# Seven-product gates in the convolution branch of a hybrid layer, between two halves of the attention branch's merging

## The chip, the cores and the metric

The kernel runs on one core of a Trainium2 chip. The metric is the device time of one execution in microseconds; the median of three runs before the change is 881.17 us. A core has TensorE (PE, matrix products, with its weight loads as PEld), VectorE (DVE), ScalarE (ACT), GpSimd (POOL), and SyncE (SP), which here only issues transfers.

## The reference

One layer on 512 positions of width 1024 (float32). Four branches read the normed input through one projection, each is gated by a sigmoid of 1024 more columns of that projection, and their sum goes through `w_o`; a gated feed-forward part with 2816 channels follows.

```python
h = rms_norm(x, mix_norm)
sc_b, sc_c, sc_x, pool_in, conf_in, q, k, v, gate_logits = split(h @ w_in)
y_sc = (sc_b * causal_dwconv(sc_c * sc_x, sc_conv)) @ sc_out
y_pool = pool_mixer(pool_in, pool_w, pool_scale)
y_conf = silu(layer_norm(causal_dwconv(a * sigmoid(g), conf_conv) + conf_conv_b, ln_g, ln_b)) @ conf_out   # a, g = split(conf_in)
y_diff = diff_attention(q, k, v, ...) @ diff_out
gates = sigmoid(gate_logits).reshape(b, s, 4, D_MODEL)
x = x + sum_i(gates_i * y_i) @ w_o
x = x + (silu(c_gate) * c_up) @ w_down      # c_gate, c_up = causal_dwconv(rms_norm(x) @ w_up)
```

## The kernel before

Activations lie transposed, 128 channels by 512 positions a tile. Each matrix operand is held as a rounded high part and the rest, and `mm3` (L181) makes one product in three: high by high, high by low (of the activation), low by high (of the weight).

**Weights.** All weights stand in one stream in the order of their use, cut into pieces of 128 x 1024 (eight 128 x 128 blocks). `fetch` (L116) loads a piece with SyncE's queue into a raw buffer, `load_chunk` (L130) splits it: ScalarE casts the high part (L144, `wh`), VectorE subtracts for the low part (L145, `wl`). Raw pieces have two buffers, split ones three, and pieces are split two ahead of use (`AHEAD`). `step` (L158) counts one unit for each block used; `at` and `after` put small work at a unit, and each `step` runs what is due.

**Seven products.** The down projection multiplies pairs of row blocks by pairs of column blocks with seven products in place of eight. The left operands are blocks of the weights (`a12, a11, a22`, from `wa`) and four sums of blocks, which GpSimd's queue adds up in DRAM with accumulating transfers (`make_sums`, L218: per group of four pieces one copy of 1 MB, then additions of 1 MB, 512 KB and 256 KB, each waiting for the one before). Such a piece ("s") has 896 columns and is loaded by two transfers, into tiles `ra` and `rb` of their own. The right operands are halves of 256 positions and combinations of them (`operands`, L707). `seven` (L729) runs the seven products of each pair, and VectorE adds the results (L755 to L758).

**Order.** TensorE's list: branch C's input, q, k, v; then the short convolution's inputs with attention's scores between; the pool inputs (GpSimd adds up windows, L567); then the four branches are merged one after the other. For branch s and d, each of eight output tiles takes `mixed` (12 products from four blocks) and `gate` (24 products of 512 columns); branch p takes 3 and 24. Branch C's 8 gates come before its outputs, 24 products each (L656), kept until its eight `mixed` (L658). Then `w_o`, and twice the feed-forward part: up projections (10, then 12 channel blocks) and the seven-product down projection.

**Between.** Branch C's convolution has 31 taps on four tiles, 124 VectorE operations (`tap`, L384, tile `cacc`) spread by units over TensorE's list. After gate 2 of branch C has begun what is left of them is issued, then `norm_mean` (L630) and, at gate 4, `norm_out` (L641): the mean and variance over channels are column sums that TensorE makes with a tile of ones (`colsum`, L319, two products each). The Tile scheduler sets each engine's list from this program order; GpSimd's is the program's order (`MANUAL`).

Of the kernel before, what the change touches and what calls it, by code (L numbers as in the profile page):

```python
# [15 lines left out]
P = 128  # L16
# [30 lines left out]
SUMU = 30  # L47
DEEP = 2
LOG_EXP = "natural_log_exp_and_others"
# [7 lines left out]
NTMP = 13  # L57
# [21 lines left out]
def hybrid_layer_kernel(ctx: ExitStack, tc: tile.TileContext, xT: bass.AP, w: bass.AP, cols: bass.AP, wa: bass.AP,  # L79
# [36 lines left out]
    def fetch(i, pieces=1):  # L116
        kind, c = plan[i]
        if kind == "s":
            g, o = divmod(c, GRP)
            ra, rb = m2(f"ra{i}", F32), m2(f"rb{i}", F32)  # L120
            nc.sync.dma_start(ra[:, :AW], wa[c])
            nc.sync.dma_start(rb, sums[g][:, o * SW:(o + 1) * SW])
            return ((slice(0, AW), ra[:, :AW]), (slice(AW, AW + SW), rb))
        raw = wp.tile([P, CW], F32, tag="raw", name=f"wr{i}", bufs=2)
        cuts = [slice(i * CW // pieces, (i + 1) * CW // pieces) for i in range(pieces)]
        for s in cuts:
            nc.sync.dma_start(raw[:, s], w[c][:, s])
        return tuple((s, raw[:, s]) for s in cuts)
# [89 lines left out]
    def make_sums():  # L218
# [11 lines left out]
        for g in range(len(sums)):  # L230
# [88 lines left out]
    def colsum(total, name):  # L319
        a = tsplit(total, name)  # L320
# [137 lines left out]
    after(QLAG, lambda: kT.extend(qk_heads("k", krows, col("k_norm"))))  # L458
    vps = time_major("v")
# [77 lines left out]
    def sc_in(j):  # L537
# [6 lines left out]
        u = padded(f"u{j}", 2)  # L544
# [44 lines left out]
    after(SUMU, make_sums)  # L589
# [33 lines left out]
    for m in range(KD):  # L623
        py = mixed(m, "d", ydiff)
        merge(m, py, gate(m, "d"))

# [3 lines left out]
    def norm_mean():  # L630
# [18 lines left out]
    for m in range(KD):  # L649
        if m == 2:  # L650
# [3 lines left out]
        if m == 4:  # L654
            norm_out()
        gates.append(gate(m, "c", True))  # L656
# [33 lines left out]
    H = T // 2  # L690
# [16 lines left out]
    def operands(i, ge, go, homes):  # L707
        def slot(name):
# [9 lines left out]
        nc.vector.scalar_tensor_tensor(  # L718
            out=wt[:, :H], in0=vt[:, :H], scalar=-1.0, in1=b22, op0=ALU.mult, op1=ALU.subtract)
        nc.vector.scalar_tensor_tensor(  # L720
            out=wt[:, H:], in0=wt[:, :H], scalar=-1.0, in1=b21, op0=ALU.mult, op1=ALU.subtract)
        v = split(vt, "", dst=(slot(f"vh{i}"), slot(f"vl{i}")))
        w_ = split(wt, "", dst=(slot(f"wh{i}"), slot(f"wl{i}")))
        left, right = slice(0, H), slice(H, T)
        pick = lambda x, c: (x[0][:, c], x[1][:, c])
        return {"b11": (e[:, left], e[:, right]), "b22": pick(o, left), "b21": pick(o, right), "v1": pick(v, left),
                "t3": pick(v, right), "w2": pick(w_, left), "t4": pick(w_, right)}

    def seven(name, ops):  # L729
        a, b, c, d = (bank(f"{name}{x}") for x in "abcd")  # L730
        r1, r6, r2, r7, r5, r4, r3 = d[:, :H], a[:, :H], a[:, H:], b[:, :H], b[:, H:], c[:, :H], c[:, H:]
        n = len(ops)
        for k, x in enumerate(ops):
            a12, a11, a22, s3_, s1_, s2_, s4_ = blocks7()
            f, l = k == 0, k == n - 1
            mm3(r1, a11, x["b11"], f, l, True)
            mm3(r5, s1_, x["v1"], f, l, True)
            mm3(r6, s2_, x["w2"], f, l, True)
            mm3(r2, a12, x["b21"], False, l, True)
# [154 lines left out]
```

## Time and profile before

| | |
|---|---|
| median of three runs | 881.17 us (880.93 to 881.26) |
| profiled execution | 880.71 us |
| its span | 878.9 us |
| TensorE busy | 871.6 us, 4372 products |
| VectorE busy | 659.3 us |
| ScalarE busy | 404.9 us |
| branch C's gate stretch | 412.35 to 456.88 us |
| first down projection | 631.48 to 681.87 us |

The span is what the profile covers, the rest of the execution lies around it. Busy time counts an instruction from its start to its end; products overlap, so the distance between two starts, and not a product's duration, tells what one costs. A wait is idle time of an engine put down to what ended it. The landing time of a transfer goes from its issue to its arrival.

### The profile page before, as it was taken

The numbers are of one execution on the slowest core, as the hardware profiler recorded it, in microseconds if no ns is written. First come the engines' busy times: TensorE is split into PE (matmuls) and PEld (weight loads), VectorE is DVE, ScalarE is ACT, GpSimd is POOL, SyncE is SP. The second block draws the span as 40 slices with busy tenths as digits, with TensorE's granted clock in tenths as the row PEclk, the third lists the DMA queues.
The fourth block names the chain that finished last, engine by engine and source line by source line (L and its number), as shares of the span: only waits on it lengthen the run. The fifth ranks groups of instructions, "written<-read, shape, count | busy, mean of one in ns | idle before, by whom it ended". The sixth has DMA issues, their size and how long they took to land.

```text
span 878.9 us, 11626 instructions
## 1 busy us (share of the span) xinstructions
PE 871.6 (99%) x4372; PEld 739.0 (84%) x4372; DVE 659.3 (75%) x1091; ACT 404.9 (46%) x636; POOL 71.3 (8%) x101
## 2 busy tenths in 40 slices
PE   9999999999999999999999999999999999999997
PEld 7888888888888888888888888888899888888997
DVE  7399966897957999534468566988886788888865
ACT  7343455464675432222564345444454344444542
POOL 1003300002411101111101100000000000000000
PEclk9999999999999999999999999999999999999999
DMA  6322242222479888888789862323662423334671
GB/s 235 114 96 97 80 123 73 72 97 97 138 200 213 183 215 206 220 216 205 189 208 250 226 157 72 119 97 103 208 178 63 131 98 97 96 106 158 174 210 49
DMA packets 54921, 128.98 MB, mean 147 GB/s; under 512 B 4896, under 2 KB 24352, under 8 KB 54688
## 3 DMA queue, kind: packets, MB, share of 16 engines
q1 hardware_dynamic: 36512, 95.98, 32.9%
q0 software_dynamic: 17776, 31.72, 18.5%
q8 instruction: 34, 0.56, 0.3%
q10 hardware_dynamic: 576, 0.53, 0.2%
q14 instruction: 23, 0.19, 0.1%
HBM read 126.12 MB, written 33.82 MB: 182 GB/s over the span
## 4 chain that ended last, share of the span: by engine, by line
PE 99%; DVE 0%; issue 0%; DVEq 0%
PE fg L182 5%; PE fu L182 5%; PE fg L183 5%; PE fu L183 5%; PE fg L184 5%; PE fu L184 5%; PE gts L182 2%; PE gts L184 2%; PE gts L183 2%; PE gtp L182 2%; PE gtc L182 2%; PE gtp L184 2%; PE gtc L183 2%; PE wo L183 2%; PE wo L182 2%; PE gtd L184 2%
## 5 line engine op out<-in xcount | busy, mean ns | idle before, releaser
L144 ACT CAST wh<-wr 128x1024 fp32r<-128x1024 f32 (+1 forms) x137 | 140.1, 1026 | 199.8 <-PE gtd L183 33.1
L145 DVE TENSOR_TENSOR wl<-wr,wh 128x1024 fp32r<-128x1024 f32 (+1 forms) x137 | 163.4, 1196 | 75.2 <-ACT wh L144 68.6
L391 DVE SCALAR_TENSOR_TENSOR cacc<-glu,colt,cacc 128x512 f32<-128x512 f32 x120 | 89.7, 752 | 1.9
L686 DVE SCALAR_TENSOR_TENSOR fc<-f,colt,fc 128x512 f32<-128x512 f32 x88 | 65.8, 749 | 7.7 <-ACT fc L684 6.4
L182 PE MATMUL fg<-hs,wh 128*128 128x512 f32 x176 | 68.5, 389 | 0.0
L184 PE MATMUL fg<-hs,wl 128*128 128x512 f32 x176 | 68.5, 389 | 0.0
L183 PE MATMUL fg<-hs,wh 128*128 128x512 f32 x176 | 68.5, 389 | 0.0
L182 PE MATMUL fu<-hs,wh 128*128 128x512 f32 x176 | 68.5, 389 | 0.0
L183 PE MATMUL fu<-hs,wh 128*128 128x512 f32 x176 | 68.5, 389 | 0.0
L184 PE MATMUL fu<-hs,wl 128*128 128x512 f32 x176 | 68.5, 389 | 0.0
L144 ACT CAST wh<-ra 128x384 fp32r<-128x384 f32 x44 | 22.6, 513 | 46.8 <-PE dn12c L183 7.6
L684 ACT ACTIVATE fc<-f,colt 128x512 f32<-128x512 f32 x44 | 31.6, 718 | 19.1 <-DVE f L103 16.6
L184 PEld LDWEIGHTS fu<-hs,wl 128*128 128x128 f32 x176 | 33.1, 188 | 6.9
L184 PEld LDWEIGHTS fg<-hs,wl 128*128 128x128 f32 x176 | 33.0, 188 | 6.9
L182 PEld LDWEIGHTS fg<-hs,wh 128*128 128x128 f32 x176 | 33.0, 188 | 6.9
L183 PEld LDWEIGHTS fg<-hs,wh 128*128 128x128 f32 x176 | 33.1, 188 | 6.8
L182 PEld LDWEIGHTS fu<-hs,wh 128*128 128x128 f32 x176 | 33.0, 188 | 6.8
L183 PEld LDWEIGHTS fu<-hs,wh 128*128 128x128 f32 x176 | 33.0, 188 | 6.8
L145 DVE TENSOR_TENSOR wl<-ra,wh 128x384 fp32r<-128x384 f32 x44 | 24.4, 554 | 19.1 <-ACT wh L144 19.0
L681 DVE TENSOR_TENSOR f<-fu,rs 128x512 f32<-128x512 f32 x22 | 15.1, 688 | 20.4 <-PE fu L184 20.4
L145 DVE TENSOR_TENSOR wl<-rb,wh 128x512 fp32r<-128x512 f32 x44 | 30.2, 687 | 0.0
L144 ACT CAST wh<-rb 128x512 fp32r<-128x512 f32 x44 | 27.1, 617 | 0.0
(1673 smaller groups left out, 2375.6 us busy)
## 6 DMA issues: line engine op xcount, KB each, us to landing
wr<-w SPq DMA_DIRECT2D x132, 512.0 KB, 3.3
sums<-s POOLq DMA_DIRECT2D x11, 1024.0 KB, 9.4
rb<-sums SPq DMA_DIRECT2D x44, 256.0 KB, 4.0
ra<-wa SPq DMA_DIRECT2D x44, 192.0 KB, 3.7
sums<-s POOLq DMA_DIRECT2D x11, 512.0 KB, 7.0
sums<-s POOLq DMA_DIRECT2D x11, 256.0 KB, 5.4
x<-xT SPq DMA_DIRECT2D x8, 256.0 KB, 5.6
xin<-xT SPq DMA_DIRECT2D x1, 1024.0 KB, 7.8
```

The source lines that it names most:

```text
L144: nc.scalar.copy(hi[:, s], src)
L145: nc.vector.tensor_tensor(out=lo[:, s], in0=src, in1=hi[:, s].bitcast(F32), op=ALU.subtract)
L182: nc.tensor.matmul(ps, a[0], b[0], start=start, stop=False, skip_group_check=shared)
L183: nc.tensor.matmul(ps, a[0], b[1], start=False, stop=False, skip_group_check=shared)
L184: nc.tensor.matmul(ps, a[1], b[0], start=False, stop=stop, skip_group_check=shared)
L391: nc.vector.scalar_tensor_tensor(out=acc31[j], in0=glus[j][:, i:i + T], scalar=wc, in1=acc31[j], op0=ALU.mult, op1=ALU.add)
L681: nc.vector.tensor_tensor(out=u[:, 2:2 + T], in0=ps, in1=rs, op=ALU.mult)
L684: nc.scalar.activation(c, u[:, 2:2 + T], AF.Copy, scale=col("ffn_conv", o + 2))
L686: nc.vector.scalar_tensor_tensor(out=c, in0=u[:, i:i + T], scalar=col("ffn_conv", o + i), in1=c, op0=ALU.mult, op1=ALU.add)
```

## The change

Branch C's gates are made in pairs by seven products of 256 columns (`gate_pair`), four pairs with four folds each. Their right operands come from the normed input: `fold` adds the high and low parts of two tiles, forms the combinations and splits them; four folds are placed by unit while the pool and attention branches are merged. The weights' sums come from four more groups in DRAM, 15 in place of 11; two of them are issued early, after k's products. All pieces now use the same raw buffers, three in place of two, the folds' sums among them, and one temporary buffer is given up. The edges of the short convolution's tiles are zeroed by VectorE, not GpSimd. In `seven` the first product of the first fold moves to the end of that fold.

The four pairs stand after four of the eight tiles of the attention branch's merging, the other four tiles after them. The mean's sum is issued 22 units after the taps' end, the variance's 14 units after the mean's. The host lays the weights out in this order.

```diff
+EARLY = 2
 DEEP = 2
+STD = 4
+FOLD = 4
+FOLDS = 14
+FOLD0 = -26
+MULAG = 22
+VARLAG = 14
+PLAN = [("n", 57 + 3 * STD // 2)]
+PLAN += [("s", MP * FOLD), ("n", 3 * (KD - STD) // 2 + 4 + 8 + 2 * CUT), ("s", MP * CUT // 2), ("n", 2 * (NP - CUT)), ("s", MP * (NP - CUT) // 2)]
...
-NTMP = 13
+NTMP = 12
...
-    up0 = w.shape[0] - 2 * NP
-    plan = [("n", c) for c in range(up0 + 2 * CUT)]
-    plan += [("s", c) for c in range(MP * CUT // 2)]
-    plan += [("n", c) for c in range(up0 + 2 * CUT, w.shape[0])]
-    plan += [("s", c) for c in range(MP * CUT // 2, MP * NP // 2)]
-    sums = [dram.tile([P, GRP * SW], F32, name=f"sums{g}") for g in range(MP * NP // 2 // GRP)]
+    plan, n_of = [], {"n": 0, "s": 0}
+    for kind, n in PLAN:
+        plan += [(kind, n_of[kind] + i) for i in range(n)]
+        n_of[kind] += n
+    sums = [dram.tile([P, GRP * SW], F32, name=f"sums{g}") for g in range(n_of["s"] // GRP)]
...
         kind, c = plan[i]
+        raw = wp.tile([P, CW], F32, tag="raw", name=f"wr{i}", bufs=3)
         if kind == "s":
             g, o = divmod(c, GRP)
-            ra, rb = m2(f"ra{i}", F32), m2(f"rb{i}", F32)
-            nc.sync.dma_start(ra[:, :AW], wa[c])
-            nc.sync.dma_start(rb, sums[g][:, o * SW:(o + 1) * SW])
-            return ((slice(0, AW), ra[:, :AW]), (slice(AW, AW + SW), rb))
-        raw = wp.tile([P, CW], F32, tag="raw", name=f"wr{i}", bufs=2)
+            n = AW + SW
+            nc.sync.dma_start(raw[:, :AW], wa[c])
+            nc.sync.dma_start(raw[:, AW:n], sums[g][:, o * SW:(o + 1) * SW])
+            return ((slice(0, n), raw[:, :n]),)
-        raw = wp.tile([P, CW], F32, tag="raw", name=f"wr{i}", bufs=2)
...
-    def make_sums():
+    def make_sums(g0, g1):
...
-        for g in range(len(sums)):
+        for g in range(g0, g1):
...
+    after(QLAG + 1, lambda: make_sums(0, EARLY))
...
-        u = padded(f"u{j}", 2)
+        u = padded(f"u{j}", 2, eng=nc.vector)
...
-    after(SUMU, make_sums)
+    after(SUMU, lambda: make_sums(EARLY, len(sums)))
...
+    hops = []
+    hhome = [x[:, i, :] for x in at_ for i in range(4)]
+
+    def fold(i):
+        def slot(name):
+            return hhome.pop(0) if hhome else m2(name)
+
+        k = slice(2 * i, 2 * i + 2)
+        f = wp.tile([P, CW], F32, tag="raw", name=f"hf{i}", bufs=3)
+        nc.vector.tensor_tensor(
+            out=f.rearrange("p (k t) -> p k t", t=T), in0=hs[:, k, 0, :].bitcast(F32),
+            in1=hs[:, k, 1, :].bitcast(F32), op=ALU.add)
+        b12, b11, b22, b21 = (f[:, j * H:(j + 1) * H] for j in range(4))
+        vt, wt = t2(f"hv{i}"), t2(f"hw{i}")
+        nc.vector.tensor_tensor(
+            out=vt.rearrange("p (b n) -> p b n", n=H), in0=f[:, H:3 * H].rearrange("p (b n) -> p b n", n=H),
+            in1=b12.unsqueeze(1).broadcast_to([P, 2, H]), op=ALU.subtract)
+        combos(vt, wt, b11, b12, b21, b22)
+        v = split(vt, "", dst=(slot(f"hvh{i}"), slot(f"hvl{i}")))
+        w_ = split(wt, "", dst=(slot(f"hwh{i}"), slot(f"hwl{i}")))
+        e, o = hs[:, 2 * i], hs[:, 2 * i + 1]
+        pick = lambda x, c: (x[:, 0, c], x[:, 1, c])
+        hops.append(table(pick(e, right), pick(o, left), pick(o, right), v, w_))
...
+            if not f:
+                mm3(r1, a11, x["b11"], f, l, True)
...
+            if f:
+                mm3(r1, a11, x["b11"], f, l, True)
...
+    def gate_pair(m, name, keep=False):
+        c11, c12, n21, n22 = seven(f"g{name}{m}", hops)
+        gs = [m2(f"sg{name}{m + i}", F32) if keep else t2(f"sg{name}{m + i}") for i in range(2)]
+        for g, c, x, scale in (
+                (gs[0], right, c11, 1.0), (gs[0], left, c12, 1.0), (gs[1], right, n21, -1.0), (gs[1], left, n22, -1.0)):
+            nc.scalar.activation(g[:, c], x, AF.Sigmoid, scale=scale)
+        return gs
...
+    for i in range(FOLD):
+        at(456 + FOLD0 + FOLDS * i, lambda i=i: fold(i))
...
-    for m in range(KD):
+    for m in range(STD):
         py = mixed(m, "d", ydiff)
         merge(m, py, gate(m, "d"))
-
     yconf = []
     gates = []
 
...
         nc.vector.tensor_tensor(out=t, in0=acc31[0], in1=acc31[1], op=ALU.add)
         for j in (2, 3):
             nc.vector.tensor_tensor(out=t, in0=t, in1=acc31[j], op=ALU.add)
-        mu = colsum(t, "mu")
+        after(MULAG, lambda a=tsplit(t, "mu"): norm_center(a))
+
+    def norm_center(a):
+        mu = ones_sum(a, "mu")
         for j in range(4):
             nc.vector.scalar_tensor_tensor(
                 out=acc31[j], in0=mu, scalar=-1.0 / 512, in1=acc31[j], op0=ALU.mult, op1=ALU.add)
             add_square(total, acc31[j], j == 0, f"cv{j}")
-
-    def norm_out():
-        rl = rsqrt(colsum(total, "var"), 1.0 / 512, t2("rl"), "rl")
+        after(VARLAG, lambda a=tsplit(total, "var"): norm_out(a))
+
+    def norm_out(a):
+        rl = rsqrt(ones_sum(a, "var"), 1.0 / 512, t2("rl"), "rl")
         for j in range(4):
             a = acc31[j]
             nc.vector.tensor_tensor(out=a, in0=a, in1=rl, op=ALU.mult)
             nc.scalar.activation(a, a, AF.Silu, scale=col("ln_g", j), bias=col("ln_b", j))
             yconf.append(split(a, f"yc{j}"))
 
-    for m in range(KD):
-        if m == 2:
+    for m in range(0, KD, 2):
+        if m == KD - 2:
             while events:
                 events.pop(0)[2]()
             norm_mean()
-        if m == 4:
-            norm_out()
-        gates.append(gate(m, "c", True))
+        gates += gate_pair(m, "c", True)
+    for m in range(STD, KD):
+        py = mixed(m, "d", ydiff)
+        merge(m, py, gate(m, "d"))```

TensorE's list where the fourth tile of the attention branch (`yd3`, `gtd3`) ends, before:

```order
L182 MATMUL gtd3_3299<-hs_104,wh62_3231 128x512
L183 MATMUL gtd3_3299<-hs_104,wh62_3231 128x512
L184 MATMUL gtd3_3299<-hs_104,wl62_3232 128x512
L182 MATMUL yd4_3336<-od0_1097,wh63_3264 128x512
L183 MATMUL yd4_3336<-od1_1098,wh63_3264 128x512
L184 MATMUL yd4_3336<-od0_1097,wl63_3265 128x512
```

The fourth tile's gate was followed by the fifth tile's output. The same place in the change (`gc0a` to `gc0d` are the result banks of the first gate pair):

```order
L190 MATMUL gtd3_3378<-hs_108,wh62_3303 128x512
L191 MATMUL gtd3_3378<-hs_108,wh62_3303 128x512
L192 MATMUL gtd3_3378<-hs_108,wl62_3304 128x512
L190 MATMUL gc0b_3417<-at0_109,wh63_3343 128x256
L191 MATMUL gc0b_3417<-at0_109,wh63_3343 128x256
L192 MATMUL gc0b_3417<-at0_109,wl63_3344 128x256
L190 MATMUL gc0a_3416<-at0_109,wh63_3343 128x256
L191 MATMUL gc0a_3416<-at0_109,wh63_3343 128x256
L192 MATMUL gc0a_3416<-at0_109,wl63_3344 128x256
```

Now the first of 336 products of 256 columns follow; the fifth tile comes after the fourth pair.

VectorE's list beside that part of TensorE's, before (`wl` is the split of a piece of weights, `sgd` and `acc` are merging):

```order
L145 TENSOR_TENSOR wl_3232<-wr_3229,wh_3231 128x1024
L601 TENSOR_TENSOR sgd_3224<-yd_3177,sgd_3224 128x512
L607 TENSOR_TENSOR acc_2228<-acc_2228,sgd_3224 128x512
L145 TENSOR_TENSOR wl_3265<-wr_3262,wh_3264 128x1024
L601 TENSOR_TENSOR sgd_3280<-yd_3228,sgd_3280 128x512
L607 TENSOR_TENSOR acc_2399<-acc_2399,sgd_3280 128x512
```

A split of a piece comes with two merging operations. In the change, around the end of the first pair (`gc0p` to `gc0s` are the additions of its results, `cacc` the taps):

```order
L153 TENSOR_TENSOR wl_3511<-wr_3449,wh_3510 128x896
L669 TENSOR_TENSOR gc0p<-gc0a,gc0s 128x512
L401 SCALAR_TENSOR_TENSOR cacc_3364<-glu_206,colt,cacc_3364 128x512
L670 TENSOR_TENSOR gc0q<-gc0b,gc0p 128x512
L153 TENSOR_TENSOR wl_3560<-wr_3478,wh_3559 128x896
L671 TENSOR_TENSOR gc0r<-gc0c,gc0q 128x512
L672 TENSOR_TENSOR gc0s<-gc0q,gc0s 128x256
L153 TENSOR_TENSOR wl_3589<-wr_3507,wh_3588 128x896
L401 SCALAR_TENSOR_TENSOR cacc_3364<-glu_206,colt,cacc_3364 128x512 x2
L153 TENSOR_TENSOR wl_3618<-wr_3556,wh_3617 128x896
```

Splits now stand between the result additions and the last taps.

GpSimd's list after k's norm, before (`kss`; `px` and `ps` are the pool branch):

```order
L415 TENSOR_TENSOR kss_909<-kss_909,half 128x8
L103 MEMSET u_1224 128x2
L103 MEMSET u_1383 128x2
L103 MEMSET u_1565 128x2
L103 MEMSET u_1743 128x2
L103 MEMSET px_1833 128x16
L567 TENSOR_TENSOR ps_1_1836<-px_1833 128x527
```

The same place in the change:

```order
L425 TENSOR_TENSOR kss_913<-kss_913,half 128x8
L234 DMA sums_81<-s 16x16384
L235 DMA sums_81<-s 512x512
L236 DMA sums_81<-s 512x256
L237 DMA sums_81<-s 512x128
L234 DMA sums_82<-s 16x16384
L235 DMA sums_82<-s 512x512
L236 DMA sums_82<-s 512x256
L237 DMA sums_82<-s 512x128
L112 MEMSET px_1845 128x16
L578 TENSOR_TENSOR ps_1_1848<-px_1845 128x527
```

Eight transfers of two groups of sums stand ahead of the pool branch, and the edges `u` have left this list.

## Rows read from the trace of the kernel before

**Rows 1.** The page: span, and busy us (share) and instructions of engines

```profile
span 878.9 us, 11626 instructions
PE   871.6 (99%) x4372; PEld 739.0 (84%) x4372; DVE 659.3 (75%) x1091; ACT 404.9 (46%) x636; POOL 71.3 (8%) x101
```

**Rows 2.** Waits of TensorE: waited for, us in total, times, longest

```profile
PE warm L269 <- DVE zeros L266: 1.5, 1, 1.5
```

**Rows 3.** Timeline of TensorE (start, us, instruction): ends of branch C's gate stretch

```profile
412.35 0.39 PE L182 MATMUL gtc<-hs,wh 128*128 128x512 f32 x1
...
456.88 0.39 PE L182 MATMUL yc<-yc0h,wh 128*128 128x512 f32 x1
```

**Rows 4.** Timeline of TensorE: ends of the first down projection

```profile
631.48 0.28 PE L182 MATMUL dn00d<-od,wh 128*128 128x256 f32 x1
...
681.87 0.40 PE L182 MATMUL fg<-hs,wh 128*128 128x512 f32 x1
```

**Rows 5.** Windows: stretch, us, busy PE, PEld, DVE, ACT, POOL, clock, DMA share, GB/s

```profile
290.00:347.00 57.00, 57.00 (x256) 47.30 (x255) 56.43 (x78) 21.23 (x26) 7.11 (x8) 1.00 0.88 210
347.00:412.35 65.35, 65.35 (x290) 54.09 (x289) 31.11 (x37) 17.04 (x21) 8.25 (x10) 1.00 0.82 203
412.35:456.88 44.53, 44.53 (x197) 36.78 (x196) 24.95 (x32) 26.32 (x37) 6.99 (x8) 1.00 0.83 210
631.48:681.87 50.39, 50.39 (x422) 50.39 (x420) 39.40 (x74) 25.49 (x50) 0.00 (x0) 1.00 0.40 120
```

**Rows 6.** Groups by line and form, VectorE and ScalarE: busy us, mean ns | idle

```profile
L145 DVE TENSOR_TENSOR wl<-wr,wh 128x1024 fp32r<-128x1024 f32 x131 | 160.7, 1227 | 74.4 <-ACT wh L144 67.8 <-PE ss L322 6.3
L391 DVE SCALAR_TENSOR_TENSOR cacc<-glu,colt,cacc 128x512 f32<-128x512 f32 x120 | 89.7, 752 | 1.9
L145 DVE TENSOR_TENSOR wl<-rb,wh 128x512 fp32r<-128x512 f32 x44 | 30.2, 687 | 0.0
L601 DVE TENSOR_TENSOR sgd<-yd,sgd 128x512 f32<-128x512 f32 x8 | 5.5, 689 | 8.0 <-ACT sgd L595 7.9
L717 DVE TENSOR_TENSOR vt<-fc,fc 128x256 f32<-128x256 f32 x11 | 4.7, 423 | 0.3
...
L144 ACT CAST wh<-wr 128x1024 fp32r<-128x1024 f32 x131 | 137.5, 1051 | 198.7 <-PE gtd L183 33.1 <-DMA wr<-w 20.5 <-PE gtp L183 15.7
L144 ACT CAST wh<-rb 128x512 fp32r<-128x512 f32 x44 | 27.1, 617 | 0.0
```

**Rows 7.** Tile `wr` between 347 and 412 us: its transfers' landing, 512 KB each

```profile
DMA to landing us min/median/max: 3.3/4.5/8.2
```

**Rows 8.** Timeline of GpSimd: a pool window, copies (L226), a step of the sums (L228)

```profile
203.05 1.10 POOL L567 TENSOR_TENSOR ps<-px 128x527 f32<-128x527 f32 x1 [25.91 <-ACT px L562]
...
386.43 0.90 POOL L226 DMA_DIRECT2D sums<-s  x1
...
412.85 0.90 POOL L226 DMA_DIRECT2D sums<-s  x1
...
479.77 1.01 POOL L228 DMA_DIRECT2D sums<-s  x1 [7.71 <-DMA sums<-s]
```

**Rows 9.** Timeline of SyncE's queue: a piece of weights, the last of four x tiles

```profile
475.84 0.33 SPq L127 DMA_DIRECT2D wr<-w  x1
...
477.64 0.43 SPq L663 DMA_DIRECT2D x<-xT  x1
```

**Rows 10.** DMA issues, 477.8 to 478.4 us: count, KB, median us to landing

```profile
x<-xT SPq DMA_DIRECT2D x1, 256.0 KB, 7.1
```

**Rows 11.** DMA issues of the whole span: second transfer of a seven-product piece

```profile
rb<-sums SPq DMA_DIRECT2D x44, 256.0 KB, 4.0
```

**Rows 12.** Timeline of ScalarE and VectorE: layer norm's variance and last split

```profile
436.09 0.68 ACT L303 ACTIVATE rlv<-var,epsc 128x512 f32<-128x512 f32 x1
...
449.52 0.69 DVE L208 TENSOR_TENSOR yc3l<-cacc,yc3h 128x512 fp32r<-128x512 f32 x1
```

More of the change, by code (lines that the diff above doesn't have):

```diff
@@ new lines, in seven, with two, twice @@
+    def seven(name, ops):
+        a, b, c, d = (bank(f"{name}{x}") for x in "abcd")
+        r1, r6, r2, r7, r5, r4, r3 = d[:, :H], a[:, :H], a[:, H:], b[:, :H], b[:, H:], c[:, :H], c[:, H:]
+        n = len(ops)
+        for k, x in enumerate(ops):
+            a12, a11, a22, s3_, s1_, s2_, s4_ = blocks7()
+            f, l = k == 0, k == n - 1
+            if not f:
+                mm3(r1, a11, x["b11"], f, l, True)
+            mm3(r5, s1_, x["v1"], f, l, True)
+            mm3(r6, s2_, x["w2"], f, l, True)
+            mm3(r2, a12, x["b21"], False, l, True)
+            mm3(r7, s3_, x["t3"], False, l, True)
+            mm3(r4, a22, x["t4"], f, l, True)
+            mm3(r3, s4_, x["b22"], False, l, True)
+            if f:
+                mm3(r1, a11, x["b11"], f, l, True)
+        s15 = t2(f"{name}s")
+        s1_, s5_ = s15[:, :H], s15[:, H:]
+        nc.scalar.copy(s1_, r1)
+        nc.scalar.copy(s5_, r5)
+        def two(x):
+            return x.rearrange("p (b n) -> p b n", n=H)
+        def twice(x):
+            return x.unsqueeze(1).broadcast_to([P, 2, H])
+        p1, p2, p3 = t2(f"{name}p"), t2(f"{name}q"), t2(f"{name}r")
+        nc.vector.tensor_tensor(out=two(p1), in0=two(a), in1=twice(s1_), op=ALU.add)
+        nc.vector.tensor_tensor(out=two(p2), in0=two(b), in1=twice(p1[:, :H]), op=ALU.add)
+        nc.vector.tensor_tensor(out=p3, in0=c, in1=p2, op=ALU.add)
+        nc.vector.tensor_tensor(out=s5_, in0=p2[:, :H], in1=s5_, op=ALU.add)
+        return p1[:, H:], p3[:, H:], p3[:, :H], s5_
@@ L818, in _layout, with gate_of @@
         tile_of(win, 12 + g)
-    for br, outs in ((0, so), (1, None), (3, do), (2, None)):
-        for m in range(KD):
-            if br == 2:
-                tile_of(win, 36 + br * 8 + m)
-                continue
-            if outs is None:
-                parts.append(pw[m // 2][:, (m % 2) * P:(m % 2 + 1) * P])
-            else:
-                tile_of(outs, m)
-            tile_of(win, 36 + br * 8 + m)
+    def gate_of(br, m):
+        tile_of(win, 36 + br * 8 + m)
+    for m in range(KD):
+        tile_of(so, m)
+        gate_of(0, m)
+    for m in range(KD):
+        parts.append(pw[m // 2][:, (m % 2) * P:(m % 2 + 1) * P])
+        gate_of(1, m)
+    for m in range(STD):
+        tile_of(do, m)
+        gate_of(3, m)
+    for m in range(STD, KD):
+        tile_of(do, m)
+        gate_of(3, m)
     for m in range(KD):
@@ L837, in _layout @@
     w = np.ascontiguousarray(stream.reshape(P, -1, CW).transpose(1, 0, 2))
[L839 removed]
+    pairs = [(win, 36 + 2 * 8 + m, k) for m in range(0, KD, 2) for k in range(FOLD)]
+    for k0, k1 in ((0, CUT // 2), (CUT // 2, NP // 2)):
+        pairs += [(dn, m, k) for m in range(0, KD, 2) for k in range(k0, k1)]
     def quads(pick):
[L842 to L843 removed]
+        a = [np.concatenate(pick(*(x[2 * k + j, :, m + i, :] for i in (0, 1) for j in (0, 1))), axis=1)
+             for x, m, k in pairs]
         return a
```

57 lines of the change are left out of this document (16 added, 41 removed).

## The prediction

> **What bounds the kernel now.** I read the busy shares first [rows 1]: TensorE works 871.6 us of the 878.9 us span, VectorE 659.3. Then the waits of TensorE [rows 2]: it waits once, 1.5 us, at the start. So TensorE never stands still, and time changes only if it gets less to do, or if the change makes it wait. Then its pace. The branch C gate stretch begins at 412.35 and the next product at 456.88 [rows 3]: 44.53 us for 192 gate products and 4 of the layer norm, 0.227 us each for 512 columns. The first half of the down projection, which already works with seven products, runs from 631.48 to 681.87 [rows 4]: 50.39 us for 4 x 5 x 21 = 420 products of 256 columns, 0.1200 us each. The three windows with these stretches show the granted clock at 1.00, the upper level of 2.4 GHz [rows 5]. A product of half the columns costs 53% of a whole one, not 50%.
>
> **Term 1, TensorE's work.** Removed: 8 gates x 8 products x 3 = 192 products of 512 columns, 192 x 0.2267 = 43.5 us (0.2267 is a run of them without layer-norm products between). Added: 4 pairs x 4 folds x 7 x 3 = 336 products of 256 columns, 336 x 0.1200 = 40.3 us. Difference: -3.2 us. The rest of TensorE's list is the same, in the same order; the four layer-norm products move behind the gates at the same size. Moving half of the attention branch's merging past the gates moves its 144 products and adds none. The Trainium skill (TensorE: Matmul & The Clock Gate, Back-to-back issue gap) gives a warm gap of N/2.4 + 2.5 ns; by that, 215.8 and 109.2 ns, an estimate from that page, the difference would be -4.7 us. The trace has a larger fixed part for this data type, so I keep -3.2.
>
> **Term 2, the cover: weights.** Every piece of weights is fetched, cast by ScalarE and subtracted by VectorE before TensorE may use it. Before, a piece serves 24 products, 5.44 us. In the new stretch a piece of 896 columns serves 21 half-width products, 2.52 us, so pieces are wanted at 2.2 times the rate. Between the rows for 512 and 1024 columns [rows 6], 896 columns cost ScalarE 0.94 and VectorE 1.09 us. Three raw buffers go round: one is free again after landing L, issue 0.3, cast 0.94 and subtraction 1.09, so a round is L + 2.3 us and must fit in three pieces, 7.56 us: L may be 5.2 us. Beyond that each of about four rounds loses L - 5.2, and a lead of about 2 us is eaten first (split pieces stand up to two ahead, 5.04 us, but of that the cast, the subtraction and VectorE's queue leave 2): **stall = 4 (L - 5.2) - 2**.
> What is L? Around that place a 512 KB piece lands in 3.3 / 4.5 / 8.2 us (least, median, most) [rows 7]; the spread goes with the sums that GpSimd's queue adds up in DRAM at the same time. These sums are still running in the new stretch: it starts where the second half of the attention merging started, 412.35 - 4 x 36 x 0.2267 = 379.7, and ends near 420, and copies start there at 386.43 and 412.85 [rows 8], since the first two of 15 groups move ahead and the third then starts where the first did. The new pieces are 448 KB, but in two transfers and with two or three in flight. The nearest row for several in flight is the burst at 475.84 [rows 9]: one 512 KB piece and four 256 KB transfers, the last issued at 477.64 and landed 7.1 us later [rows 10], with a step of the sums issued into it at 479.77 [rows 8]. That is 1.5 MB in 8.9 us, or 2.6 us per 448 KB with the fixed latency of the first in it. The rate just suffices for 2.52. Without sums, the 256 KB half lands in 4.0 us [rows 11]. Bounds for L: 4.0 and 8.2, so the stall is between 0 and 10 us. I take L = 5.4, a little above the median of single landings; the stall is then 0, and I put 0.6 for single late landings.
>
> **Term 3, VectorE.** From the start of the first pair to the end of the fourth, the order leaves VectorE 14 subtractions of 896 columns and 2 of 1024 (17.7 us), 11 taps of the convolution that the folds pushed back (8.3), four times three 512-wide and one 256-wide addition of the seven results (4 x 2.49 = 10.0), four 512-wide operations for the mean (2.8) and two for merging (1.4): 40.1 us beside 40.3 us of TensorE [durations from rows 6]. That is full, where the down projection loads VectorE 39.40 of 50.39 [rows 5]. It fits as long as VectorE never waits: between 290 and 347 it is busy 56.43 of 57 us and TensorE doesn't wait there either [rows 5, 2]. The wait that I count in at most 1.2 us deep is the one in front of each pair's second addition, where subtraction of the next piece is queued behind three result additions.
>
> **Edits at no time.** The folds cost VectorE four times about 4.2 us (one 1024-wide, one 512-wide, two 256-wide operations and two splits) while the pool and attention branches are merged; they displace taps, and nobody waits for taps before the mean. The early sums (8 transfers on GpSimd's queue) lie ahead of the pool branch's small GpSimd work; k's products end after 128 units of 0.68 us, near 93 us, the sums are issued 25 units later, near 110, and two groups at 26 us each, the distance of the copies, end near 162, before that work at 203.05 [rows 8]. What they would block, the zeroing of four edges, moves to VectorE, 4 x 0.06 us. The mean's products get 22 units and the variance 14. From the variance to the branch's output there are 81 products, 18.4 us. Before, ScalarE reads the variance at 436.09 and the branch's last split begins at 449.52 [rows 12]; with its 0.69 us and 1 us from the product to the read that chain is 15 us. With one table load more (1.3 us in this trace) it ends 2 us ahead. If this cover is gone, TensorE waits for the overhang alone, 1 to 2 us. The down projection's 44 pieces lose their own buffers and share the three raw ones: L = 4.0 with no sums beside them is under 5.2, so 0.
>
> **Sum.** The profiled execution took 880.71 us (span 878.9 and 1.8 around it): 880.71 - 3.2 + 0.6 = 878.1. It lies 0.46 below the median 881.17; against the median the time is 878.5. What can be told from no change is 0.2%, 1.76 us: faster means under 879.4, so a stall up to 1.4; slower means above 882.9, a stall over 5.
>
> **Rivals.** (a) *VectorE is the bound* and passes single late landings on. The sum of 40.1 in 40.3 has no room to catch up. A landing of 8.2 in place of 5.2 idles VectorE 3 us; two copies fall into the stretch, 6 us, less the lead of 2: a stall of 4, time 881.17 - 3.2 + 4 = 882.0, no difference to be seen. For it: the full list. Against it: the subtractions' pipelined starts lie some 0.08 us under their durations, which gives back 2 to 3 us over the stretch. (b) *The weights' queue is the bound, and the time is worse than before.* If all landings rise with the doubled demand to 7.2 us, each round is 9.5 us in place of 7.56, and the stall is 4 x 2 - 2 = 6 us: 884.0. It decides from L = 6.95 on. For it: single landings already reach 8.2 with half the demand, and 203 GB/s are moved at a share of 0.82 [rows 5]. Against it: the burst's 2.6 us per piece. The Trainium skill (DMA: Bandwidth & Descriptors, Queues, rings and completion order) says that each DMA engine takes turns between queues, a packet at a time, which would make weights share with the sums as (b) has it; the spread of the landings agrees with it. (c) *A wait elsewhere*: one temporary buffer fewer (12 for 13), GpSimd's queue filled early, or the three shared buffers in the down projection, where 44 pieces at 0.1 us each would be 4.4 us: 882.4.
>
> **How the numbers follow.** Forecast (stall 0 to 1.4): 0.52. (a), stall 1.4 to 5: 0.25. (b): 0.15. (c): 0.08, half of it within 0.2% and half slower. So faster 0.52, same 0.29, slower 0.19. Forecast's own range: 877.9 to 879.4. The range for 8 in 10 starts at no stall, 877.8, and reaches to the lower part of (b), 883.4.
>
> **What would show it.** Right: TensorE's gate rows start 0.120 us apart, the stretch from the first of them to the next merging product is 40.3 to 41 us, TensorE has no wait on the weights' split there, and landings stay at or under 5.2 us. Wrong: TensorE waits for a split; if ScalarE's cast waited for the landing it is (b), if VectorE's subtraction came straight behind other work of VectorE it is (a). Term 1 is wrong if the half-width products don't start 0.120 us apart with these operands.

## The result, and the profile after

The changed kernel takes 886.39 us (median of four runs, 885.10 to 887.29), the kernel before in the same series 881.05: a ratio of 1.0059 with a 95% interval of 1.0042 to 1.0077. It is slower by 5.3 us, where 878.5 was predicted, and lies outside the range (877.8 to 883.4).

The page of the changed kernel, to be held against [rows 1]:

```profile
span 885.5 us, 12011 instructions
...
PE 872.6 (99%) x4516; PEld 745.1 (84%) x4516; DVE 686.0 (77%) x1099; ACT 415.4 (47%) x625; POOL 85.3 (10%) x113
```

TensorE's busy time should have gone down by 3.2 us. It went up from 871.6 to 872.6, and the span grew by 6.6. So two things happened: TensorE stood still for some us, and it was also busy longer than its products should take. The waits of TensorE between 379 and 430 us, the branch C gate stretch, show the first; before, TensorE had no wait there [rows 2]:

```profile
PE gc6d L190 <- ACT wh L152: 3.1, 1, 3.1
PE gc4b L190 <- ACT wh L152: 1.0, 1, 1.0
PE gc4b L192 <- DVE wl L153: 0.6, 1, 0.6
PE gc6d L192 <- DVE wl L153: 0.3, 1, 0.3
```

All four are waits for the two halves of a piece of weights. The windows of the changed kernel (length; busy time and count of PE, PEld, DVE, ACT and POOL; granted clock; DMA share; GB/s) show the second. They answer to [rows 5]: the whole gate stretch, a part of it, and the first down projection.

```profile
379.86:429.12 49.26, 44.19 (x338) 42.95 (x337) 33.83 (x45) 20.77 (x36) 7.13 (x8) 0.93 0.97 251
418.46:424.36 5.90, 5.56 (x24) 5.27 (x25) 5.80 (x8) 3.61 (x8) 0.17 (x1) 0.50 0.93 181
637.00:688.00 51.00, 50.84 (x421) 50.52 (x420) 36.97 (x55) 23.40 (x32) 0.00 (x0) 1.00 0.56 170
```

The stretch took 49.26 us in place of the predicted 40.3 to 41, and for 5.90 us of it the granted clock was 0.50, that is 1.2 GHz. The transition into that part, in TensorE's timeline (start, duration, what; in brackets the wait and its releaser):

```profile
415.13 0.28 PE L192 MATMUL gc6d<-hs,wl 128*128 128x256 f32 x1
418.46 0.58 PE L190 MATMUL gc6d<-hs,wh 128*128 128x256 f32 x1 [3.06 <-ACT wh L152]
418.84 0.41 PE L191 MATMUL gc6d<-hs,wh 128*128 128x256 f32 x1
419.59 0.58 PE L192 MATMUL gc6d<-hs,wl 128*128 128x256 f32 x1 [0.33 <-DVE wl L153]
419.97 0.41 PE L190 MATMUL gc6b<-at,wh 128*128 128x256 f32 x1
420.18 0.41 PE L191 MATMUL gc6b<-at,wh 128*128 128x256 f32 x1
```

Up to 415.13 products start 0.120 us apart, as Term 1 wanted. Then TensorE stops for 3.3 us, and the next products of the same form start 0.21 us apart (419.97 to 420.18). What ended the stop is read one engine further back. ScalarE's timeline and then VectorE's at the same place:

```profile
417.47 0.94 ACT L152 CAST wh<-wr 128x896 fp32r<-128x896 f32 x1 [6.40 <-DMA wr<-sums]
```

```profile
418.44 1.09 DVE L153 TENSOR_TENSOR wl<-wr,wh 128x896 fp32r<-128x896 f32 x1 [6.25 <-ACT wh L152]
```

ScalarE had been idle for 6.40 us until the piece landed, VectorE for 6.25 us until ScalarE's cast. So the chain is transfer, cast, subtraction, product; no engine was full. The landing of the transfers that bring the gates' pieces in the stretch (least, median, most, in us; a gate piece comes by two and is there when both have landed) and the two queues' packets, bytes and share of the 16 DMA engines' time there (q1 carries SyncE's weights, q0 GpSimd's sums):

```profile
DMA to landing us min/median/max: 4.2/5.8/9.2
```

```profile
q0 software_dynamic: 2704, 5.24, 53.2%
q1 hardware_dynamic: 3858, 7.07, 43.3%
```

A transfer took 4.2 / 5.8 / 9.2 us to land, against 3.3 / 4.5 / 8.2 for whole pieces of 512 KB before [rows 7]. For the four pieces in a row that were issued between 404.9 and 412.6, on which the long stop hangs, the landing was:

```profile
DMA to landing us min/median/max: 4.3/7.4/9.2
```

Their second transfers landed after 4.7, 9.2, 8.1 and 7.0 us. Two other transfers were issued just ahead of the one that took 9.2: 256 KB of a tile of `x` on SyncE's own queue, and a group's copy of 1 MB on GpSimd's:

```profile
406.25 0.33 SPq L761 DMA_DIRECT2D x<-xT  x1
407.47 0.90 POOL L234 DMA_DIRECT2D sums<-s  x1
```

The transfer of `x` alone does not make a stop: the two kernels below that have no wait in this stretch issue it there as well, at 400.99 and 403.81. How much it adds beside the sums was not tested.

**Where the 9 us went.** All this is the profiled execution, at 887.29 us the longest of the four. Without any wait the stretch takes 40.31 us (the first experiment below). The change loses 8.95 us against that: 2.64 before the fourth pair's second fold, most of it in two stops between 400.07 and 402.52 (that fold should have begun at 412.61 and could have at 415.25); 3.21 in the stop itself, 415.25 to 418.46; and 3.10 behind it, since the last 63 products took 10.66 us (418.46 to 429.12) in place of 63 x 0.120 = 7.56. Of these 3.10, 0.33 is a wait, and 2.77 is the lower clock. So some 6.2 us are waits and 2.8 are clock. (The list of waits above adds up to 5.0, since it counts idle time only; the 6.2 are counted from start to start and hold the slow starts next to each stop.)

### The profile page after: what moved, and what is told of

It is laid out like the page before. It is cut to its first block, busy times and chain, and to the rows that moved or that the text cites. A ratio compares the mean times of both kernels' runs of the same rounds, so it can differ in the third digit from the quotient of the medians.

```text
span 885.5 us, 12011 instructions
## 1 busy us (share of the span) xinstructions
PE 872.6 (99%) x4516; PEld 745.1 (84%) x4516; DVE 686.0 (77%) x1099; ACT 415.4 (47%) x625; POOL 85.3 (10%) x113
## 4 chain that ended last, share of the span: by engine, by line
PE 96%; DMA 2%; DVE 1%; ACT 0%; issue 0%; DVEq 0%; SPq 0%; ACTq 0%
PE fg L191 5%; PE fu L191 5%; PE fg L192 5%; PE fu L192 5%; PE fg L190 5%; PE fu L190 4%; PE gts L190 2%; PE gts L192 2%; PE gts L191 2%; PE wo L192 2%; PE gtd L190 2%; PE gtp L191 2%; PE gtd L191 2%; PE wo L190 2%; PE gtp L190 2%; PE gtd L192 2%
## 5 line engine op out<-in xcount | busy, mean ns | idle before, releaser
L152 ACT CAST wh<-wr 128x1024 fp32r<-128x1024 f32 (+2 forms) x189 | 188.1, 998 | 241.2 <-issue 27.3
L153 DVE TENSOR_TENSOR wl<-wr,wh 128x1024 fp32r<-128x1024 f32 (+2 forms) x189 | 218.9, 1162 | 78.0 <-ACT wh L152 70.7
L401 DVE SCALAR_TENSOR_TENSOR cacc<-glu,colt,cacc 128x512 f32<-128x512 f32 x120 | 90.7, 756 | 2.3
L190 PE MATMUL fg<-hs,wh 128*128 128x512 f32 x176 | 68.5, 389 | 0.0
L191 PE MATMUL fg<-hs,wh 128*128 128x512 f32 x176 | 68.5, 389 | 0.0
L192 PE MATMUL fg<-hs,wl 128*128 128x512 f32 x176 | 68.5, 389 | 0.0
L190 PE MATMUL fu<-hs,wh 128*128 128x512 f32 x176 | 68.5, 389 | 0.0
L191 PE MATMUL fu<-hs,wh 128*128 128x512 f32 x176 | 68.5, 389 | 0.0
L192 PE MATMUL fu<-hs,wl 128*128 128x512 f32 x176 | 68.5, 389 | 0.0
L190 PEld LDWEIGHTS fu<-hs,wh 128*128 128x128 f32 x176 | 33.0, 188 | 6.9
L190 PEld LDWEIGHTS fg<-hs,wh 128*128 128x128 f32 x176 | 33.0, 188 | 6.9
L191 PEld LDWEIGHTS fg<-hs,wh 128*128 128x128 f32 x176 | 33.0, 188 | 6.8
L191 PEld LDWEIGHTS fu<-hs,wh 128*128 128x128 f32 x176 | 33.0, 188 | 6.8
L192 PEld LDWEIGHTS fg<-hs,wl 128*128 128x128 f32 x176 | 33.0, 188 | 6.8
L192 PEld LDWEIGHTS fu<-hs,wl 128*128 128x128 f32 x176 | 33.0, 188 | 6.8
L236 POOL DMA_DIRECT2D sums<-s x15 | 15.2, 1013 | 143.6 <-DMA sums<-s 143.6
L501 ACT ACTIVATE p<-p,st 128x128 f32<-128x128 f32 (+3 forms) x32 | 17.7, 555 | 16.8 <-DVE st L498 16.6
L190 PE MATMUL gts<-hs,wh 128*128 128x512 f32 x64 | 25.4, 397 | 0.0
L799 ACT ACTIVATE fc<-fc 128x512 f32<-128x512 f32 x22 | 13.9, 630 | 24.2 <-DVE fc L784 23.6
## 6 DMA issues: line engine op xcount, KB each, us to landing
wr<-sums SPq DMA_DIRECT2D x60, 256.0 KB, 3.8
sums<-s POOLq DMA_DIRECT2D x15, 256.0 KB, 4.9
x<-xT SPq DMA_DIRECT2D x8, 256.0 KB, 4.7
```

The costliest lines, as they stand in the source:

```text
L152: nc.scalar.copy(hi[:, s], src)
L153: nc.vector.tensor_tensor(out=lo[:, s], in0=src, in1=hi[:, s].bitcast(F32), op=ALU.subtract)
L190: nc.tensor.matmul(ps, a[0], b[0], start=start, stop=False, skip_group_check=shared)
L191: nc.tensor.matmul(ps, a[0], b[1], start=False, stop=False, skip_group_check=shared)
L192: nc.tensor.matmul(ps, a[1], b[0], start=False, stop=stop, skip_group_check=shared)
L236: lambda g: nc.gpsimd.dma_start(view(g, 2, 4), src(s2, g, 2), accum_op=ALU.add),
```

## The experiments

Two theories were put against each other. T1: the transfers that add up the weights' sums in DRAM delay the gates' pieces, TensorE stops for them, and its clock falls after the long stop (rival b of the prediction, with the clock added). T2: VectorE's list is full and passes lateness on (rival a). A third question was whether the other edits cost anything (rival c). Each group of experiments was timed beside the kernel before, which had medians of 881.17, 880.81, 880.91 and 880.78 us.

### The sums held back

```diff
+HOLD = 7
...
-    after(SUMU, lambda: make_sums(EARLY, len(sums)))
+    after(SUMU, lambda: make_sums(EARLY, HOLD))
...
         gates += gate_pair(m, "c", True)
+    held = sm.tile([P, 16], F32, tag="edge", name="held")
+    nc.gpsimd.tensor_tensor(out=held, in0=gates[-1][:, :16], in1=gates[-1][:, :16], op=ALU.add)
+    make_sums(HOLD, len(sums))
```

> Groups 7 to 14 of the weights' sums in DRAM are issued only when the eight gates are finished; groups 2 to 6 as before, so that no sums are moved in the gate stretch. T1 (the sums' transfers slow the weights' landings, the missing weights stop TensorE, and its clock falls after the stop): pieces land in at most 5.5 us there, no wait of TensorE on a split there, stretch from the first gate product to the next merging product 40.3 to 41.0 us in place of 49.3, granted clock 1.00, time 877.8 to 879.0 us. T2 (VectorE is full and passes on its lateness): the stretch stays above 45 us and the time at 884 to 887. Between the two (880 to 883) a part of the wait has another source.

Measured: 877.63 us (877.34 to 877.83), ratio 0.9957 (0.9940 to 0.9973). TensorE has no wait in the stretch. Its window and the landing of the pieces:

```profile
379.70:420.01 40.31, 40.31 (x338) 40.31 (x336) 36.22 (x48) 22.73 (x38) 0.00 (x0) 1.00 0.60 183
```

```profile
DMA to landing us min/median/max: 2.3/3.2/4.4
```

All 8.95 us are back, and the pieces' transfers land in 3.2 us in the median in place of 5.8. The time is 0.2 us under the expected range. VectorE has the same list as in the change and is busy 36.22 of 40.31 us without making TensorE wait. This kernel beats both the kernel before and the change. T1 holds, T2 falls.

### VectorE relieved

```diff
-    for n, (j, i) in enumerate(taps):
+    for n, (j, i) in enumerate(taps[:-17]):
```

> The last 17 of the 124 taps of branch C's convolution are left out of the computation, so VectorE has about 13 us less to do just before and in the gate stretch; the sums are moved as in the change. T1 (late weights): ScalarE's cast still waits 4 to 6 us for landings, the stretch stays at 46 to 50 us, time 884 to 887. T2 (VectorE full): the stretch falls to 40.3 to 42 us, time 878 to 880.

Measured: 884.14 us (881.46 to 886.82, eight runs). In the profiled execution the stretch took 44.40 us. ScalarE still waits for landings, between 379 and 430 us (total, times, longest):

```profile
ACT wh L152 <- DMA wr<-sums: 17.4, 6, 5.0
```

The wait on transfers stays with VectorE's load gone, so T2 falls here as well. The stretch is shorter than the expected 46 to 50. In this execution TensorE's stops were at most 1.0 us each, and the granted clock stayed at 1.00. The eight runs spread over 5.4 us, and with the clock: the three with a mean granted clock of 0.998 or 0.999 over the whole run took 881.46 to 883.09 us, the five with 0.994 to 0.997 took 884.07 to 886.82. Why the stops are shorter here was not shown. The edit moved one more thing: the transfer of `x` goes at 375.39, ahead of the stretch, where in the change it goes at 406.25.

### Four raw buffers

```diff
-MID = 35
+MID = 33
...
-        raw = wp.tile([P, CW], F32, tag="raw", name=f"wr{i}", bufs=3)
+        raw = wp.tile([P, CW], F32, tag="raw", name=f"wr{i}", bufs=4)
...
-        f = wp.tile([P, CW], F32, tag="raw", name=f"hf{i}", bufs=3)
+        f = wp.tile([P, CW], F32, tag="raw", name=f"hf{i}", bufs=4)
```

> Four raw buffers in place of three (two fewer of the buffers for mid-sized tiles). A round of four pieces is 10.1 us, so a landing may take 7.8 us before TensorE has to wait. T1 in the form that the latency of single pieces counts: of the landings of the stretch only two are later than 7.8, the waits fall under 2 us together, the clock stays up, time 878 to 880.5. T1 in the form that the bandwidth beside the sums is short: the landings grow with one more in flight (median from 5.8 to over 7 us), the waits stay, time 883 to 887. T2 (VectorE full): 884 to 887, and the cast does not wait for landings.

Measured: 877.97 us (877.95 to 880.21; three runs at 877.95 to 877.97, two at 879.68 and 880.21), ratio 0.9970 (0.9957 to 0.9983). The profiled execution, of 877.95, has no wait of TensorE in the stretch. The stretch, its landings, and its queues:

```profile
379.95:420.47 40.52, 40.52 (x338) 40.42 (x337) 34.26 (x46) 21.36 (x36) 5.71 (x7) 1.00 1.00 273
```

```profile
DMA to landing us min/median/max: 3.5/5.9/9.7
```

```profile
q1 hardware_dynamic: 3586, 6.80, 50.1%
q0 software_dynamic: 2183, 4.21, 49.1%
```

The transfers land as late as in the change (5.9, at most 9.7), but one more piece is on its way, and that covers it. The weights get 6.80 MB in 40.52 us, 168 GB/s, where in the change they got 7.07 in 49.26, 144 GB/s; the sums run on at 104 in place of 106. So the bandwidth that three buffers left unused was there: 273 GB/s in place of 251. The form of T1 in which the bandwidth itself is short is refuted; what was short is how many pieces were asked for ahead of time.

### The copy in short rows

```diff
-            lambda g: nc.gpsimd.dma_start(sums[g], s0[g]),
+            lambda g: nc.gpsimd.dma_start(sums[g], s0[g], max_dma_last_dim=GRP * SW),
```

> The 1 MB copy that begins each group of sums is cut into rows of 2048 floats, 128 of them, like the addition after it, in place of long ones; bytes and order are the same. If the copy's long packets are what holds the weights' packets up: the worst landings in the stretch fall from 9 us to about 6, the waits with them to under 2 us, time 878.5 to 881. If the bytes themselves count: landings and the time as in the change, 884 to 887.5. T2 (VectorE full): no change as well, 884 to 887.5.

Measured: 887.63 us (886.25 to 888.59); the transfers land as late as before the edit:

```profile
DMA to landing us min/median/max: 4.3/6.5/9.4
```

The form of the copy gave nothing back here.

### Plain copies in place of the sums

On the kernel with the sums held; `COPIES` is 5, then 2.

```diff
+    sink = dram.tile([P, GRP * SW], F32, name="sink")
+    begun = sm.tile([P, 16], F32, tag="edge", name="begun")
+    nc.gpsimd.tensor_tensor(out=begun, in0=acc[STD - 1][:, :16], in1=acc[STD - 1][:, :16], op=ALU.add)
+    for i in range(COPIES):
+        nc.gpsimd.dma_start(sink, s0[i])
```

> On the kernel with the sums held, five plain copies of 1 MB inside DRAM, one after the other on GpSimd's queue, are issued when the gate stretch begins; nobody needs their result, and they add nothing up. If bytes beside the weights are what delays the weights: landings of the gates' pieces rise from 3.2 to 5 us or more in the median, TensorE waits again, stretch 43 to 50 us, time 880.5 to 887. If only accumulating transfers do it: landings stay under 4 us, time 877.3 to 878.5.

> As with the five plain copies, but only two, so that the second ends some 15 us into the gate stretch. If the loss follows the bytes moved beside the weights: late landings in the first 15 us only, which the split pieces that stand ready absorb in part; a wait of 0 to 2 us, time 877.6 to 880. If a loss of the same size as with five copies (887.0) comes, it isn't the bytes but the presence of such a transfer.

Measured: 887.0 us (886.67 to 888.58) with five, 879.59 (879.23 to 881.00) with two, 877.63 with none. The stretch is 49.02, 41.81 and 40.31 us long. With five copies, the stretch, its queues, and the pieces' landing:

```profile
379.71:428.73 49.02, 42.81 (x338) 40.85 (x336) 35.44 (x48) 21.20 (x36) 3.44 (x6) 1.00 0.77 250
```

```profile
q1 hardware_dynamic: 3810, 6.97, 48.2%
q0 software_dynamic: 160, 5.24, 28.7%
```

```profile
DMA to landing us min/median/max: 2.4/5.8/8.1
```

Five copies move the same 5.24 MB beside the weights as the sums did, add nothing up, and bring the loss back in full. The first of them is issued at 386.08, 6 us into the stretch. With two copies, the second issued at 391.31, the stretch loses 1.5 us: 1.2 by 402 and 0.3 near 406.5. (The profiled execution of that kernel, at 881.00 the longest of its ten, has two more waits, of 0.8 and 0.4 us, for operands of the first down projection.) So it is the bytes on another queue, not the adding, and with none, two and five copies the loss grows with their number.

### One piece delayed, no transfer late

Again on the kernel with the sums held. `MORE` is 2, 4 and 7: piece 72, in the third pair, is cast that many times more.

```diff
-                    nc.scalar.copy(hi[:, s], src)
+                    for _ in range(1 + (MORE if c == 72 else 0)):
+                        nc.scalar.copy(hi[:, s], src)
```

> On the kernel with the sums held (877.63 us, no wait in the gate stretch) one piece of the third gate pair is cast three times in place of once, which delays its subtraction once. By the times of that kernel's trace TensorE then waits once for about 1.0 us (0.3 to 1.8). If TensorE's clock falls only after a longer stop: granted clock 1.00 throughout, time 878.2 to 879.4, so the loss is the wait. If any stop drops the clock: products 0.21 us apart behind it, time 881 or more.

> The same with five casts in place of one, a single wait of about 4.2 us (3.3 to 5). If the clock falls after a stop of such length, as the trace of the change suggests: granted clock 0.50 behind it for about 6 us, products 0.21 us apart there, so 3 to 3.7 us more on top of the wait, time 884 to 886.5. If the clock had fallen in the change for another reason: clock 1.00, time 881 to 882.5.

> The kernel with the sums held, with one piece of the third gate pair cast eight times in place of once, so that TensorE stands still once, for 4 to 5 us, with no transfer late. If a single stop of that length drops the clock, as the trace of the change suggests: products 0.21 us apart and a granted clock of 0.50 for about 6 us behind it, 3 to 3.7 us on top of the wait, time 884.5 to 886.5. If the clock stays at 1.00 the loss is the wait alone: 881.5 to 882.8, and the fall in the change needs another reason.

The first two missed their wait: I had assumed that ScalarE would stand still between the casts for the second pair's results, and it didn't, so two more casts were absorbed (877.58 us, 877.44 to 881.58, no wait), and four more made TensorE stop for 0.72 us only (878.37 us, 877.88 to 879.42; the clock stayed at 1.00). The third did what it should: 884.46 us (884.17 to 885.73). TensorE's timeline at the stop, and the window behind it:

```profile
402.37 0.28 PE L195 MATMUL gc4d<-hs,wl 128*128 128x256 f32 x1
407.23 0.39 PE L193 MATMUL gc4d<-hs,wh 128*128 128x256 f32 x1 [4.58 <-ACT wh L155]
407.45 0.28 PE L194 MATMUL gc4d<-hs,wh 128*128 128x256 f32 x1
407.57 0.38 PE L193 MATMUL gc4b<-at,wh 128*128 128x256 f32 x1
407.75 0.41 PE L194 MATMUL gc4b<-at,wh 128*128 128x256 f32 x1
```

```profile
407.57:411.06 3.49, 3.49 (x17) 3.21 (x16) 2.73 (x3) 0.45 (x1) 0.00 (x0) 0.51 0.41 105
```

One stop with no sums in flight is enough: shortly after TensorE resumes, the granted clock is at 0.50, products start 0.21 us apart, and it is back at 411. The stretch took 46.84 us, 6.53 more than without the stop: 4.74 for the stop and 1.8 for the clock. I had expected 3 to 3.7, since I took the 5.9 us at half clock from the change; here it lasted 3.5. This execution is the shortest of the four: its mean granted clock is 0.996, that of the other three 0.994 and 0.995, which points to a longer fall there.

### Eight products in the new place

The gates as before, 24 products of 512 columns each, where the change has the pairs; no folds, no sums for the gates, everything else as in the change. Then the same with four raw buffers.

```diff
...
-    for m in range(0, KD, 2):
+    for m in range(KD):
...
-        gates += gate_pair(m, "c", True)
+        gates.append(gate(m, "c", True))
...
```

> Branch C's gates in eight products of 512 columns as in the kernel before, but in the new place, with the early sums, the three shared raw buffers, the 12 temporary ones and the later norm as in the change; no folds, 11 groups of sums. T1: half the demand for weights, so no wait beside the sums; TensorE has 3.2 to 3.5 us more to do than with seven products: time 880.7 to 881.6, the gate stretch 43.5 us. If one of the other edits costs time (rival c of the prediction): above 882.5.

> Branch C's gates in eight products in the new place (882.25 us, with a wait of 0.8 us for a weight's split in the fourth pair of the first down projection), now with four raw buffers in place of three. If that wait comes from the three raw buffers that the down projection shares (rival c of the prediction): the wait goes, time 880.8 to 881.5, the same as the kernel before. If it comes from VectorE's queue of result additions alone: the wait stays, time 881.8 to 882.8.

Measured: 882.25 us (881.39 to 882.86) with three raw buffers, 880.88 (880.76 to 881.51) with four; the latter has a ratio of 1.000 to the kernel before (0.9991 to 1.0010). The gate stretch is 43.52 us in both. With three buffers TensorE waits once in the first down projection:

```profile
PE dn03d L192 <- DVE wl L153: 0.8, 1, 0.8
```

So the new place, the early sums, the later norm and the 12 temporary buffers cost nothing that can be measured. The three raw buffers, shared with the down projection, cost 1.4 us between the medians of these two kernels (rival c, in small), of which the wait accounts for 0.8; in the change itself that wait is 0.2 us.

### Both remedies

The held sums and the four raw buffers together, the two edits above.

> Both remedies at once: sums held until the gates are done, and four raw buffers (two fewer of the mid-sized ones). T1: neither kernel alone has a wait left in the gate stretch, so together they give no more than either: 877.2 to 878.0 us. Below 877 would mean that waits were left which the traces did not show.

Measured: 877.50 us (877.26 to 878.61), ratio 0.9965 (0.9952 to 0.9978). As expected, no more than either alone.

## Why the prediction was wrong

**Term 1 was right.** Half-width products start 0.120 us apart with these operands, and the stretch takes 40.31 us where nothing waits. In the same place eight products take 43.52 us, 3.2 more, as predicted. In time, between the two kernels with four raw buffers and the sums not held, eight products take 880.88 us and seven 877.97: 2.9 us; with the sums held as well, seven take 877.50. The forecast of 878.5 is, to 0.9 us, the time of the kernel without the sums' traffic (877.63).

**Term 2 failed, at L.** The mechanism and its place were rival (b), to which I gave 0.15, and the step that failed was "I take L = 5.4" with a stall of 0 behind it; the waits measured some 6.2 us. Rival (b) put L at 7.2 for all landings and got 6.0 us. That the two agree so closely is luck: the median landing was 5.8, for which the formula gives 0.4 us, and the loss came in two places.

Two things went wrong in the step. First, a median was the wrong number. The late pieces came next to each other (9.2, 8.1 and 7.0 us for three in a row), and with three buffers a run of late pieces is what counts. Second, I read the burst in [rows 9, 10] as a rate that "just suffices", with a step of the sums issued into it, and not as a landing. An addition of 1 MB, issued at 471.05, had run beside it from its start, until the step at 479.77 followed. GpSimd's line, the queues between 475.84 and 484.75, and the landing of the burst's four transfers of 256 KB, all before the change:

```profile
471.05 1.01 POOL L227 DMA_DIRECT2D sums<-s  x1 [6.50 <-DMA sums<-s]
```

```profile
q0 software_dynamic: 590, 0.87, 58.7%
q1 hardware_dynamic: 720, 1.57, 47.7%
```

```profile
DMA to landing us min/median/max: 6.6/6.8/7.1
```

So SyncE's queue got 1.57 MB in 8.91 us, 176 GB/s, beside the sums, close to the 182 that the pairs want. But in the burst five transfers were asked for at once, and four of them took 6.6 to 7.1 us each, above the 5.2 that three buffers allow. With 7.1 as L, high perhaps, since five were in flight, the formula gives 5.6 us.

The windows gave a warning as well. Before, 203 GB/s took a share of 0.82 [rows 5], and the sums' queue had 97 GB/s of that between 347 and 412 us:

```profile
q0 software_dynamic: 3760, 6.29, 52.7%
```

With the pairs' 182 that is 279, and in proportion 0.82 x 279 / 203 = 1.13 of the engines' time, an estimate. The proportion is rough: with four buffers 273 GB/s stood at a share of 1.00, where it gives 1.10, and TensorE did not wait. It warned that little room was left; three buffers could not ask in time for what there was.

The Trainium skill (DMA: Bandwidth & Descriptors, Queues, rings and completion order), which the prediction named beside rival (b), says that a DMA engine takes turns between the queues that have work for it, a packet at a time. That weights fall behind as soon as another queue has work (median landing 3.2 us alone, 5.8 beside the sums) agrees with it. From it I would then expect long packets of the other queue to hurt more, and the runs do not settle that: the plain copies came in 160 packets, the sums in 2704, and all the pieces' transfers together gave a median landing of 5.8 us beside either; the 256 KB transfers alone gave 6.7 us beside the copies and 5.8 beside the sums, but the sums also add.

**The clock was not in the prediction at all.** It made 2.8 of the 9 us that the stretch lost in the profiled execution. Even rival (b) priced a wait at its own length. It is not the whole loss: the mean granted clock of the four runs was 0.994 (887.29 and 887.18 us), 0.996 (885.61) and 0.998 (885.10), where the kernel before has 0.998 to 1.000. So one run of the change shows no fall of that size, and it is still 4.0 us slower than the kernel before; the waits alone make the change a loss, and the clock adds some 2 us where it falls. The experiment with one delayed piece shows that a single stop of 4.9 us brings the fall with no transfer late; stops up to 1.0 us, in the profiled run with fewer taps, and up to 2.1 us, in that with five copies, did not. The Trainium skill (TensorE: Matmul & The Clock Gate, HAM oscillation — how this bites in real kernels) states that a wait for data between bursts of products can drop the clock so that the next burst starts slow. The trace agrees, at 0.50 behind the stop. With it a long stall is dearer than it is long, and the prediction left that out.

**Term 3 and rival (a).** My sum of 40.1 us of VectorE's work was too high: VectorE is busy 36.22 of 40.31 us in the kernel without waits. The difference, 3.9 us, is about what the 0.08 us make that a start lies under a duration (48 operations, 3.8 us), which the prediction named under (a) and left out of the sum. In this stretch VectorE follows the casts and delays nobody.

**Edits at no time.** Right for the early sums, the moved zeroing and the norm, as the eight products in the new place show. That kernel has no folds; for them it is the kernel with both remedies, which gains 3.4 us against it, no less than the 3.2 of TensorE's work. For the three raw buffers in the down projection the 0 was not quite right (0.2 us in the change, and up to 1.4 us with other gates).

## What to carry to other kernels

When an edit makes an engine consume its operands faster, add up the GB/s that the stretch then wants together with whatever else is moving there, and compare it with the share that the same traffic takes now. Then ask how long a landing the buffers can cover, and take L from the row with as much in flight beside the same traffic; a median of single landings hides the run of late pieces that empties the buffers. If there is little room, move the traffic that can wait, or ask for one more piece ahead of time: either gave back the loss here and left the change 3 us faster than the kernel before. Price a stall of TensorE of several us above its length, since the products behind it ran at half the clock for 3.5 to 5.9 us.

## What the runs showed of the hardware that I had not expected

The share of the DMA engines' time does not tell how late another queue's transfers get: the sums filled 53.2% of it and the plain copies 28.7%, for the same 5.24 MB and the same median landing of 5.8 us; the rate was alike, 251 and 250 GB/s in all.

A fourth piece in flight raised what the DMA engines moved from 251 to 273 GB/s with hardly any loss to the other queue (106 to 104 GB/s), though the engines' share had already stood at 0.97.

The time at half clock differed: 5.9 us after the stop of 3.3 us in the change, where a shorter stop lay 13 us ahead and a wait of 0.33 us fell into it, and 3.5 us after the single stop of 4.9 us. In the kernel with the copy in short rows, whose stops fall alike, it was 5.8 us behind a stop of 3.5. What sets it stays open. In the kernel with five copies the nine stops of the profiled execution's stretch, the longest 2.11 us from start to start, made 7.7 of the 8.7 us that it lost, and the window of the stretch shows a clock of 1.00; the other three runs of that kernel have a mean granted clock of 0.995 to 0.997, where this one has 0.998.
